# Where the operand sums of the second token half are formed, in a hybrid decoder layer

## The chip, the cores and the metric

One core of a Trainium2 chip runs the whole layer. The metric is the device time of one execution in microseconds (us). The program gives work to five engines, each of which takes its own instructions in order: PE (TensorE, the matmuls), DVE (VectorE), ACT (ScalarE), POOL (GpSimd) and SP (SyncE, which issues most transfers here). Transfers, once issued, run on DMA engines beside all of them.

## What is computed

A decoder layer on 2048 tokens of width 1024, all in float32: a norm, an input projection, two recurrent mixers, an output projection with residual, a second norm, a feed-forward block with residual, and a last norm. Only the feed-forward block matters here:

```python
D_MODEL = 1024; SEQ = 2048; D_FF = 2816; CONV_WIDTH = 3
def _conv_ffn(h, w_up, conv_w, conv_b, w_down):
    u = h @ w_up                                   # (2048, 1024) @ (1024, 5632)
    u = lax.conv_general_dilated(u, conv_w[:, None, :], window_strides=(1,),
        padding=[(CONV_WIDTH - 1, 0)], ..., feature_group_count=C) + conv_b
    gate, val = jnp.split(u, 2, axis=-1)
    return (jax.nn.silu(gate) * val) @ w_down      # (2048, 2816) @ (2816, 1024)
# in the layer:
x = x + _conv_ffn(_rmsnorm(x, norm2_w[l]), w_up[l], conv_w[l], conv_b[l], w_down[l])
return _rmsnorm(x, final_norm_w)
```

## The kernel before

**Products in three parts.** Each float32 operand is split into a rounded high part (an ACT cast, L244 or L237) and the rest (a DVE subtraction, L245 or L238). A product of two operands is three matmuls per tile (`mm3`, L258 to L262), so each operand costs PE nothing and ACT and DVE one pass each.

**Seven products for eight.** Both projections of the feed-forward block multiply 2 by 2 blocks with seven products instead of eight. This needs sums and differences of blocks as operands. Four sums are made from four tiles with four DVE operations, each using the one before.

**Up-projection.** `run` (L1324) goes through 2 token halves with 22 row groups of the hidden width each: iterations n = 0 to 43, and 44 which only finishes. An iteration has seven products (`prod`, L1344) of 12 matmuls on 128 by 512 tiles. The last two of an iteration (`late`, L1398) are done after the first product of the next iteration, and then the convolution and the gate follow. The gated product of row group fb, `y`, is stored to DRAM by two transfers (L1423) into `gd_[2h]` and `gd_[2h+1]`, one per block of 512 tokens. Weights come through six buffers named `uraw`, split operands through five named `uwh` and `uwl`.

**Work on the side.** `side` is a list of small pieces: loads, DVE operations with their stores, and empty pauses. `aside` (L1290) takes one piece after each product, seven per iteration. `four` (L1250) appends a group of five pieces: load four tiles (`raw_`, six buffers named `br`), pause, two DVE operations, two DVE operations and four stores, pause. The pieces made so are the norm of the later tokens, sums of the hidden state, sums of the down-projection's weights (`Tw`), and from iteration 23 on the sums of the first token half's gated product: 11 row groups (KH = 11), each reading rows kk and 11+kk of `gd_[0]` and `gd_[1]` and writing row group kk of the four tensors `Sg[0][0..3]`.

**Down-projection.** `steps` lists 143 steps (half g, product p, row group kk), each 12 matmuls on two operands of 128 by 512, 256 KB each. The first three run at the end of the up-projection (`down_start`). In the loop from L1489, step s issues the loads for step s+4 (six buffers named `draw`), splits the operands of step s+2 and does its matmuls. At the end of each product results are added to the residual rows `xt3`, which are loaded ahead (L1449), and finished rows are normalised and stored to `out` (L1465). The loads and stores all stand in SP's queue, in order. The second half's products read `Sg[1]`. Its sums are made in the same loop:

```python
sums_at = {KH + 5 * j + 2: j for j in range(KH)}
...
            if s_ in sums_at:
                g_sums(d_raw("sraw"), 1, sums_at[s_])
```

`g_sums` (L191) loads four tiles into six buffers named `sraw`, does the four DVE operations (L194 to L197) and issues four stores (L199). The steps are 13, 18, ... 63; steps 66 on belong to the second half, and `Sg[1]` is read from its second product on.

A scheduling layer puts the instructions of each engine into a fixed order when the program is built, and sets the waits from what each reads and writes, DRAM tensors too. PE's products keep the code's order; loads and vector operations may move against each other.

Of the kernel before, what the change touches and what calls it, by code (L numbers as in the profile page):

```python
# [21 lines left out]
KD = D // P  # L22
# [3 lines left out]
NFF = FF // P  # L26
# [35 lines left out]
def tile_layer(ctx, tc, consts, x, norm1_w, w_in, hg_lb_logits, hg_norm_w, rw_shift_mu, rw_w0, rw_w2,  # L62
# [5 lines left out]
    dma = nc.sync.dma_start  # L68
# [25 lines left out]
    def pst(name):  # L94
        return pools["ps"].tile([P, 512], F32, tag="mm", name=name, bufs=8)
# [39 lines left out]
    with tc.tile_pool(name="vp", bufs=1, reuse_waits="tile") as vp, tc.tile_pool(name="ps0", bufs=1, space=PSUM, reuse_waits="tile") as pools["ps"]:  # L135
        rows = vp.tile([P, P], F32, name="rows")
        V.memset(rows, 0.0)
        n = 0
# [39 lines left out]
    h2d = [dp.tile([D, BLK], F32, name=f"h2d{b}") for b in range(NBLK)]  # L178
    gd_ = [dp.tile([FF, BLK], F32, name=f"gd{b}") for b in range(NBLK)]
    KH = NFF // 2  # L180
    Sg = [[dp.tile([KH * P, BLK], F32, name=f"Sg{g}{i}") for i in range(4)] for g in range(2)]
    Tw = [dp.tile([KH * P, BLK], F32, name=f"Tw{i}") for i in range(4)]

    def krows(t_, q, kk):

        return t_[(q * KH + kk) * P:(q * KH + kk + 1) * P, :]

# [3 lines left out]
    def g_sums(tile_, g, kk):  # L191
# [6 lines left out]
        for i, t_ in enumerate((a22, a11, a21, a12)):  # L198
# [4 lines left out]
          ("b", 3, (1, 1)))  # L203
    steps = [(g, p, kk) for g in range(2) for p in range(7) for kk in range(KH) if (g, p) != (0, 1)]
    M2 = [dp.tile([P, BLK], F32, name=f"M2{i}") for i in range(4)]
# [7 lines left out]
    def d_matmuls(accs, s_, lhs, rhs, i):  # L213
        g, p, kk = steps[s_]
        is_ = slice(i * P, (i + 1) * P)
        mm3(accs[i], (lhs[0][:, is_], lhs[1][:, is_]), rhs, kk == 0 and p in (0, 1, 3), kk == KH - 1, True)
    Ts = [[dp.tile([BLK, BLK], F32, name=f"Ts{h}{i}") for i in range(4)] for h in range(2)]
# [40 lines left out]
    def mm3(acc, lhs, rhs, first, last, skip=False):  # L258
        (lh, ll), (rh, rl) = lhs, rhs
        TE.matmul(acc, lh, rh, start=first, stop=False, skip_group_check=skip)  # L260
        TE.matmul(acc, lh, rl, start=False, stop=False, skip_group_check=skip)  # L261
        TE.matmul(acc, ll, rh, start=False, stop=last, skip_group_check=skip)  # L262
# [844 lines left out]
    with ExitStack() as c2:  # L1107
# [11 lines left out]
        def raw_(src):  # L1119
            t_ = hr.tile([P, BLK], F32, tag="br", name="br", bufs=6)  # L1120
            if src is not None:
                loader[0](t_, src)
            return t_
# [20 lines left out]
        with tc.tile_pool(name="op", bufs=1, reuse_waits="tile") as op_:  # L1144
# [46 lines left out]
            for dh in range(2):  # L1191
                accs = [pst("wacc") for _ in range(4)]
                for n, k in enumerate((0, 1, 4, 5, 2, 3, 6, 7)):
# [16 lines left out]
                    if dh == 1 and 2 <= n:  # L1210
                        for j in range(2):
                            q = 2 * (n - 2) + j
# [9 lines left out]
        with tc.tile_pool(name="up", bufs=1, reuse_waits="tile") as up:  # L1222
# [2 lines left out]
            V.memset(halo, 0.0)  # L1225


            side = []

            def norm_last(b, i2):  # L1230

                xt = []

                def load():
                    for q in range(2):
                        xt.append(up.tile([P, D], F32, tag="xt2", name="xt2", bufs=2))
                        dma(xt[q], x1d[b][(i2 * 2 + q) * P:(i2 * 2 + q + 1) * P, :])

                def scale(q):
                    V.tensor_scalar_mul(xt[q], xt[q], rstd(hr, xt[q], "nst", "br", 6))  # L1240

                def evict(k, tp, w):
                    t_ = hr.tile([P, 256], F32, tag="br", name="h2", bufs=6)
                    act(t_, tp, AF.Copy, scale=w)
                    dma(h2d[b][k * P:(k + 1) * P, i2 * 256:i2 * 256 + 256], t_)

                g = transposed(xt, "n2", lambda: pst("tp"), evict)
                side.extend([load, None, lambda: scale(0), lambda: scale(1), None] + [lambda: next(g)] * KD)

            def four(srcs, make, dsts):  # L1250

                ts = []
                side.extend([lambda: ts.extend(raw_(v) for v in srcs), None,
                             lambda: make(ts, 0), lambda: (make(ts, 1), [dma(d, t_) for d, t_ in dsts(ts)]), None])

            def t_make(ts, part):
                b11, b12, b21, b22 = ts
# [16 lines left out]
            QB = [(q, b) for q in range(2) for b in range(2)]  # L1274
            t_out = lambda row: lambda ts: [(row(i), ts[j]) for i, j in enumerate((0, 3, 1, 2))]
            s_out = lambda row: lambda ts: [(row(i), ts[j]) for i, j in enumerate((3, 0, 2, 1))]
# [3 lines left out]
            for kk in range(4):  # L1280
                four([hsrc(1, q, b, kk) for q, b in QB], t_make, t_out(lambda i, kk=kk: tdst(1, i, kk)))
            for kk in range(KH):
                four([wd_quarter(q, dh, kk) for q, dh in QB], t_make, t_out(lambda i, kk=kk: krows(Tw[i], 0, kk)))
            late_side = len(side)
            for kk in range(KH):
                four([krows(gd_[u], q, kk) for u, q in QB], s_make, s_out(lambda i, kk=kk: krows(Sg[0][i], 0, kk)))
            side.reverse()
            late_side = len(side) - late_side

            def aside(n):  # L1290

                if side and (1 <= n < NFF - 2 or n > NFF) and (n > NFF or len(side) > late_side):
                    f = side.pop()
                    if f is not None:
                        f()

# [132 lines left out]
    with tc.tile_pool(name="dn", bufs=1, reuse_waits="tile") as dn:  # L1429
        ops, xts, pend, m2 = {}, {}, [], {}  # L1430
        N = len(steps)

        def d_raw(tag):
            def f(src):
                t_ = dn.tile([P, BLK], F32, tag=tag, name=tag, bufs=6)
                dma(t_, src)
                return t_
            return f

        raws = {}  # L1440

        def load(s_):
            if s_ < N and s_ not in raws:
                g, p, kk = steps[s_]
                raws[s_] = d_loads(s_, d_raw("draw"))
                if p == 0 and kk in (4, 6, 8, 10) or p == 2 - g and kk in (1, 3, 5, 7):
                    u, i = (0, kk // 2 - 2) if p == 0 else (1, kk // 2)
                    t_ = dn.tile([P, D], F32, tag="xt3", name="xt3", bufs=12)
                    dma(t_, x1d[2 * g + u][i * P:(i + 1) * P, :])  # L1449
                    xts[(g, u, i)] = t_  # L1450

        def take(s_):
            if s_ < N:
                ops[s_] = (split(dn, raws[s_][0], [P, BLK], "da", 5), split(dn, raws[s_][1], [P, BLK], "db", 5))
                raws.pop(s_)

        def add(g, u, dh, i, acc):
            t_ = xts[(g, u, i)][:, dh * BLK:(dh + 1) * BLK]
            V.tensor_add(t_, acc, t_)

        def finish(g, u, i):
            t_ = xts.pop((g, u, i))
            V.scalar_tensor_tensor(t_, t_, rstd(dn, t_, "fst"), fw, ALU.mult, ALU.mult)
            t0 = (2 * g + u) * BLK + i * P
            dma(out[0, t0:t0 + P, :], t_)  # L1465

        def evict(g, p, accs, i):

            if p in (0, 2, 4):
                add(g, *((0, 0), None, (0, 1), None, (1, 1))[p], i, accs["a"][i])  # L1470
            if p == 1:
                pend.append(lambda: add(g, 0, 0, i, accs["b"][i]))
            if p == 4:
                pend.append(lambda: add(g, 1, 1, i, accs["b"][i]))
            if p == 5:
                pend.append(lambda: (add(g, 1, 0, i, accs["a"][i]), finish(g, 1, i)))
            if p == 6:
                pend.append(lambda: (add(g, 0, 1, i, accs["b"][i]), finish(g, 0, i)))

        fw = None  # L1480
        accs = {"a": dstate["accs"]}
        for s_ in range(3, 7):
            load(s_)
        take(3)
        take(4)
        fw = dn.tile([P, D], F32, name="fw")
        dma(fw, final_norm_w.unsqueeze(0).broadcast_to([P, D]))
        sums_at = {KH + 5 * j + 2: j for j in range(KH)}
        for s_ in range(3, N):  # L1489
            g, p, kk = steps[s_]  # L1490
            if "b" not in accs and p == 3:
                accs["b"] = [pst("db") for _ in range(4)]
            load(s_ + 4)
            take(s_ + 2)
            acc = accs[DP[p][0]]
            if s_ < N - 3:
                lhs, rhs = ops.pop(s_)
                for i in range(4):
                    d_matmuls(acc, s_, lhs, rhs, i)
                    if kk == KH - 1:  # L1500
                        evict(g, p, accs, i)
            elif s_ == N - 1:
                for i in range(4):
                    for q in range(N - 3, N):
                        d_matmuls(acc, q, *ops[q], i)
                    evict(g, p, accs, i)
            if pend and kk != KH - 1:
                pend.pop(0)()
            if (g, p) == (0, 2):
                if kk == 0:  # L1510
                    for i in range(4):
                        m2[i] = dn.tile([P, BLK], F32, tag="m2", name="m2", bufs=4)
                        dma(m2[i], M2[i])
# [37 lines left out]
```

## Time and profile before

| | us |
|---|---|
| median of 3 runs | 2756.31 (2747.66 to 2756.97) |
| profiled execution | 2742.4 |
| its span, first to last instruction | 2740.6 |
| PE busy | 2638.4 (96%) |
| DVE busy | 1899.1 (69%) |
| ACT busy | 1349.5 (49%) |

The page's 40 slices of 68.5 us each, in tenths of busy time, and what the transfers moved:

```profile
PE   7999999989999999999899999999999999998998
DVE  4857656575456664757568789988898787667656
DMA  8655544355653546933674467746763222999865
```

The up-projection runs from about slice 21 to slice 34, the down-projection from slice 34 to the end. A digit of PE does not mean peak: a matmul of 128 by 512 is shown some 390 ns long, while the next one starts earlier. In the views of groups, a line like L244 or L1436 belongs to a helper and holds many tiles; the names before and after the arrow (`draw<-Sg`) tell which.

### The profile page before, as it was taken

To read this page: it belongs to the slowest core of one execution; us is meant where nothing else is said; L and a number is where in the kernel's file an instruction comes from. 1 tells how busy PE (TensorE), PEld (TensorE's weight loads), DVE (VectorE), ACT (ScalarE), POOL (GpSimd) and SP (SyncE) were. 2 spreads that over 40 slices of the span, in tenths; PEclk is the share of its full clock that TensorE was granted. 3 is DMA by queue.
4 is the path that set the end of the run, shared out by engine and by line. 5 is a ranking of instruction groups with operands and counts; after the bars stand their busy time and mean duration, and the time that the engine had idled before them with its cause. 6 is when DMAs were issued, how large, how long until landed. Compare 5 with 4: busy or idle time off the path is not lost.

```text
span 2740.6 us, 47945 instructions
## 1 busy us (share of the span) xinstructions
PE 2638.4 (96%) x18059; PEld 2098.8 (77%) x18059; DVE 1899.1 (69%) x3665; ACT 1349.5 (49%) x2168; POOL 368.9 (13%) x660
## 2 busy tenths in 40 slices
PE   7999999989999999999899999999999999998998
PEld 6777777767777767778677888887888888776887
DVE  4857656575456664757568789988898787667656
ACT  5455443444544444443356754556445554445544
POOL 6433222212222113222100000000000000000000
PEclk9999999999999999999999999999999999999999
DMA  8655544355653546933674467746763222999865
GB/s 303 199 166 166 165 136 130 117 148 183 214 167 111 148 152 204 311 123 119 182 265 139 140 199 258 240 148 207 264 232 113 90 86 76 323 333 327 298 194 184
DMA packets 365437, 517.87 MB, mean 189 GB/s; under 512 B 97439, under 2 KB 194069, under 8 KB 365205
## 3 DMA queue, kind: packets, MB, share of 16 engines
q1 hardware_dynamic: 313265, 345.39, 38.9%
q0 software_dynamic: 51872, 169.41, 19.0%
q8 instruction: 142, 2.33, 0.4%
q14 instruction: 90, 0.74, 0.1%
q10 hardware_dynamic: 68, 0.02, 0.0%
HBM read 376.27 MB, written 138.41 MB: 188 GB/s over the span
## 4 chain that ended last, share of the span: by engine, by line
PE 68%; DMA 10%; DVE 8%; issue 6%; ACT 5%; SPq 1%; POOL 1%; DVEq 0%; ACTq 0%; POOLq 0%
PE pj L260 8%; PE pj L261 7%; PE pj L262 7%; PE ua L262 5%; PE ua L260 5%; PE ua L261 5%; PE ud L262 2%; PE ud L260 2%; PE ud L261 2%; PE da L261 2%; PE da L260 2%; PE da L262 2%; PE hg L971 2%; DMA woraw<-in_w_out_dram 2%; PE ub L262 1%
## 5 line engine op out<-in xcount | busy, mean ns | idle before, releaser
L260 PE MATMUL pj<-hh,wh 128*128 128x512 f32 x960 | 403.5, 420 | 1.4 <-ACT hh L117 0.7
L261 PE MATMUL pj<-hl,wh 128*128 128x512 f32 x960 | 379.5, 396 | 0.0
L262 PE MATMUL pj<-hh,wl 128*128 128x512 f32 x960 | 379.2, 395 | 0.0
L260 PE MATMUL ua<-Bh,uwh 128*128 128x512 f32 x704 | 276.8, 393 | 4.9 <-ACT uwh L244 3.1
L262 PE MATMUL ua<-Bh,uwl 128*128 128x512 f32 x704 | 275.1, 391 | 0.2 <-DVE uwl L245 0.2
L261 PE MATMUL ua<-Bl,uwh 128*128 128x512 f32 x704 | 274.7, 390 | 0.0
L260 PEld LDWEIGHTS pj<-hh,wh 128*128 128x128 f32 x960 | 181.7, 189 | 54.7 <-issue 11.8
L261 PEld LDWEIGHTS pj<-hl,wh 128*128 128x128 f32 x960 | 182.0, 190 | 39.4 <-issue 6.2
L262 PEld LDWEIGHTS pj<-hh,wl 128*128 128x128 f32 x960 | 181.6, 189 | 39.8 <-issue 0.4
L244 ACT CAST uwh<-uraw 128x512 fp32r<-128x512 f32 x220 | 134.1, 617 | 124.6 <-PE ua L261 58.5
L245 DVE TENSOR_TENSOR uwl<-uraw,uwh 128x512 fp32r<-128x512 f32 x220 | 147.0, 686 | 48.7 <-ACT uwh L244 48.5
L244 ACT CAST dah<-draw 128x512 fp32r<-128x512 f32 x140 | 87.0, 622 | 184.7 <-DMA draw<-Sg 60.0
L245 DVE TENSOR_TENSOR dal<-draw,dah 128x512 fp32r<-128x512 f32 x140 | 96.6, 690 | 103.8 <-ACT dah L244 103.5
L260 PEld LDWEIGHTS ua<-Bh,uwh 128*128 128x128 f32 x704 | 132.6, 188 | 33.6 <-ACT uwh L244 3.5
L262 PEld LDWEIGHTS ua<-Bh,uwl 128*128 128x128 f32 x704 | 132.5, 188 | 28.4 <-DVE uwl L245 0.6
L261 PEld LDWEIGHTS ua<-Bl,uwh 128*128 128x128 f32 x704 | 132.7, 188 | 27.0
L260 PE MATMUL ud<-Bh,uwh 128*128 128x512 f32 x352 | 137.9, 392 | 0.3 <-ACT uwh L244 0.3
L262 PE MATMUL ud<-Bh,uwl 128*128 128x512 f32 x352 | 137.1, 390 | 0.0
L261 PE MATMUL ud<-Bl,uwh 128*128 128x512 f32 x352 | 137.0, 389 | 0.0
L261 PE MATMUL da<-dbl,dah 128*128 128x512 f32 x340 | 133.3, 392 | 1.3 <-DVE dbl L245 1.3
L262 PE MATMUL da<-dbh,dal 128*128 128x512 f32 x340 | 132.3, 390 | 0.0
L260 PE MATMUL da<-dbh,dah 128*128 128x512 f32 x340 | 124.6, 392 | 6.5 <-ACT dbh L244 6.5
(570 smaller groups left out, 6050.3 us busy)
## 6 DMA issues: line engine op xcount, KB each, us to landing
uraw<-in_w_up_dram SPq DMA_DIRECT2D x176, 256.0 KB, 3.4
woraw<-in_w_out_dram POOLq DMA_DIRECT2D x96, 256.0 KB, 3.5
draw<-Sg SPq DMA_DIRECT2D x88, 256.0 KB, 3.4
draw<-Tw SPq DMA_DIRECT2D x88, 256.0 KB, 3.4
gd<-y SPq DMA_DIRECT2D x86, 256.0 KB, 3.0
xt<-x1d SPq DMA_DIRECT2D x32, 512.0 KB, 7.2
wraw<-in_w_in_dram POOLq DMA_DIRECT2D x60, 256.0 KB, 4.7
br<-in_w_down_dram SPq DMA_DIRECT2D x58, 256.0 KB, 3.8
```

The source lines that it names most:

```text
L244: S.copy(hi, src)
L245: V.tensor_sub(lo, src, hi.bitcast(F32))
L260: TE.matmul(acc, lh, rh, start=first, stop=False, skip_group_check=skip)
L261: TE.matmul(acc, lh, rl, start=False, stop=False, skip_group_check=skip)
L262: TE.matmul(acc, ll, rh, start=False, stop=last, skip_group_check=skip)
L971: TE.matmul(o, kt[:, t0:t0 + 64], qs, start=True, stop=True, tile_position=(0, e * 64))
```

## The change

Eight of the 11 row groups of the second half's sums (`EARLY = 8`, row groups 0 to 7) become pieces on the side in the up-projection, one group per iteration from n = 35 to 42. Row group kk needs rows kk and 11+kk of `gd_[2]` and `gd_[3]`; row 11+kk is stored during iteration 34+kk, and the group starts at 35+kk. For this each piece on the side carries the first iteration in which it may run. The other three groups stay in the down-projection, at steps 13, 19 and 25. The four operations, four loads and four stores of a group are the same in both places, with `br` buffers instead of `sraw`.

```diff
+    EARLY = 8
...
-            side = []
+            side, first_at = [], [1]
+
+            def aside_of(fs):
+
+                side.extend((first_at[0], f) for f in fs)
...
-                side.extend([lambda: ts.extend(raw_(v) for v in srcs), None,
-                             lambda: make(ts, 0), lambda: (make(ts, 1), [dma(d, t_) for d, t_ in dsts(ts)]), None])
+                aside_of([lambda: ts.extend(raw_(v) for v in srcs), None,
+                          lambda: make(ts, 0), lambda: (make(ts, 1), [dma(d, t_) for d, t_ in dsts(ts)]), None])
...
-            late_side = len(side)
-            for kk in range(KH):
-                four([krows(gd_[u], q, kk) for u, q in QB], s_make, s_out(lambda i, kk=kk: krows(Sg[0][i], 0, kk)))
+            for g in range(2):
+                for kk in range(({0: KH, 1: EARLY})[g]):
+                    first_at[0] = NFF + 1 + g * (KH + 1 + kk)
+                    four([krows(gd_[2 * g + u], q, kk) for u, q in QB], s_make,
+                         s_out(lambda i, g=g, kk=kk: krows(Sg[g][i], 0, kk)))
             side.reverse()
-            late_side = len(side) - late_side
...
-                if side and (1 <= n < NFF - 2 or n > NFF) and (n > NFF or len(side) > late_side):
-                    f = side.pop()
+                if side and n >= side[-1][0] and not NFF - 2 <= n <= NFF:
+                    f = side.pop()[1]
...
-        sums_at = {KH + 5 * j + 2: j for j in range(KH)}
+        sums_at = {KH + 6 * j + 2: EARLY + j for j in range(KH - EARLY)}
```

The order of PE's instructions does not change. Three places where others move; lines after the change are some five higher than before.

DVE in iteration 35 of the up-projection, from the split of `s1` (an operand) to the convolution of the iteration before (`y1`, `y0`). Before:

```order
L245 TENSOR_TENSOR uwl_21759<-s1_21736,uwh_21758 128x512
L245 TENSOR_TENSOR uwl_21776<-uraw_21644,uwh_21775 128x512
L1415 SCALAR_TENSOR_TENSOR y1_21707<-cv_21561,cvt_14639,y1_21707 128x1024
L1407 TENSOR_TENSOR cg_21560<-ud_21563,m2_21601 128x512
L1416 SCALAR_TENSOR_TENSOR y1_21707<-cv_21561,cvt_14639,y1_21707 128x1024
```

Now:

```order
L246 TENSOR_TENSOR uwl_21769<-s1_21744,uwh_21768 128x512
L1273 TENSOR_TENSOR br_21671<-br_21669,br_21671 128x512
L1274 TENSOR_TENSOR br_21669<-br_21665,br_21669 128x512
L246 TENSOR_TENSOR uwl_21792<-uraw_21644,uwh_21791 128x512
L1276 TENSOR_TENSOR br_21665<-br_21671,br_21665 128x512
L1421 SCALAR_TENSOR_TENSOR y1_21715<-cv_21561,cvt_14639,y1_21715 128x1024
L1413 TENSOR_TENSOR cg_21560<-ud_21563,m2_21601 128x512
L1422 SCALAR_TENSOR_TENSOR y1_21715<-cv_21561,cvt_14639,y1_21715 128x1024
L1277 TENSOR_TENSOR br_21667<-br_21667,br_21665 128x512
```

The four operations of a group (`br`) stand between the splits and inside the convolution; what was there before keeps its order. The first of them waits for the loads of its tiles, and all behind it waits with it.

SP at the same place, around the store of row 11 of the gated product (`gd2`, `gd3` from `y0_21547`). Before:

```order
L1139 DMA uraw_21797<-in_w_up_dram 128x4x128
L1423 DMA gd2_156<-y0_21547 128x512
L1423 DMA gd3_157<-y0_21547 128x512
L1139 DMA uraw_21799<-in_w_up_dram 128x4x128
```

Now:

```order
L1140 DMA uraw_21813<-in_w_up_dram 128x4x128
L1429 DMA gd2_156<-y0_21547 128x512
L1429 DMA gd3_157<-y0_21547 128x512
L1140 DMA uraw_21815<-in_w_up_dram 128x4x128
L1123 DMA br_21667<-gd2_156 128x512
L1123 DMA br_21669<-gd3_157 128x512
L1123 DMA br_21671<-gd3_157 128x512
L1123 DMA br_21836<-gd2_156 128x512
L1259 DMA Sg10_162<-br_21671 128x512
L1259 DMA Sg12_164<-br_21669 128x512
L1140 DMA uraw_21817<-in_w_up_dram 128x4x128
L1259 DMA Sg11_163<-br_21665 128x512
```

The loads of the group follow the store of the row that two of them read, with one weight load between, and a weight load stands behind the stores of the sums.

SP in the down-projection, at the sixth product of the first half (`gd1` with `Tw3`). Before, with one of the groups of sums:

```order
L1436 DMA sraw_24325<-gd2_156 128x512
L1436 DMA sraw_24327<-gd2_156 128x512
L1436 DMA sraw_24329<-gd3_157 128x512
L1436 DMA sraw_24331<-gd3_157 128x512
L1436 DMA draw_24341<-gd1_155 128x512
L1436 DMA draw_24343<-Tw3_169 128x512
L1436 DMA draw_24366<-gd1_155 128x512
L1436 DMA draw_24368<-Tw3_169 128x512
L199 DMA Sg10_162<-sraw_24331 128x512
L199 DMA Sg11_163<-sraw_24325 128x512
L199 DMA Sg12_164<-sraw_24329 128x512
L199 DMA Sg13_165<-sraw_24327 128x512
```

Now:

```order
L1455 DMA xt3_25156<-x1d2_148 128x1024
L1442 DMA draw_24377<-gd1_155 128x512
L1442 DMA draw_24379<-Tw3_169 128x512
L1442 DMA draw_24405<-gd1_155 128x512
L1442 DMA draw_24407<-Tw3_169 128x512
L1442 DMA draw_24430<-gd1_155 128x512
L1442 DMA draw_24432<-Tw3_169 128x512
```

Operand loads follow one another, and the loads of the second half's first residual rows (`xt3` from `x1d2`) have moved ahead of the output stores, which they stood among before.

More of the change, by code (lines that the diff above doesn't have):

```diff
@@ L1247, in norm_last @@
                 g = transposed(xt, "n2", lambda: pst("tp"), evict)
-                side.extend([load, None, lambda: scale(0), lambda: scale(1), None] + [lambda: next(g)] * KD)
+                aside_of([load, None, lambda: scale(0), lambda: scale(1), None] + [lambda: next(g)] * KD)
             def four(srcs, make, dsts):
                 ts = []
-                side.extend([lambda: ts.extend(raw_(v) for v in srcs), None,
-                             lambda: make(ts, 0), lambda: (make(ts, 1), [dma(d, t_) for d, t_ in dsts(ts)]), None])
+                aside_of([lambda: ts.extend(raw_(v) for v in srcs), None,
+                          lambda: make(ts, 0), lambda: (make(ts, 1), [dma(d, t_) for d, t_ in dsts(ts)]), None])
             def t_make(ts, part):
```

## The prediction

> **What bounds the kernel now.** I read the busy time by stage first, because the page's 96% for PE is a mean over stages that differ. Stretches of the last part, in us from the span's start (columns: PE, PEld, DVE and ACT busy time with instruction counts, POOL, granted clock, DMA share, GB/s):
>
> ```profile
> 2330.00:2400.00 70.00, 66.24 (x286) 53.28 (x286) 46.40 (x71) 32.35 (x52) 1.11 (x2) 1.00 0.91 327
> 2400.00:2480.00 80.00, 78.69 (x339) 62.67 (x338) 56.96 (x89) 35.07 (x56) 0.00 (x0) 1.00 0.94 333
> 2480.00:2560.00 80.00, 71.42 (x295) 55.27 (x294) 56.09 (x82) 41.73 (x84) 0.00 (x0) 0.98 0.94 338
> 2560.00:2720.00 160.00, 160.00 (x707) 132.49 (x706) 94.82 (x145) 75.17 (x138) 0.00 (x0) 1.00 0.68 219
> ```
>
> The down-projection is PE-bound from 2560 on and transfer-bound before. The count of matmuls shows the loss better than the busy time, since a matmul is shown 389 ns long but follows its predecessor sooner. The spacing comes from an up-projection iteration, and the row under it is the stretch in which the up-projection already forms sums, those of the first half:
>
> ```profile
> 2142.12:2161.16 19.04, 19.04 (x86) 15.77 (x85) 14.78 (x22) 9.69 (x15) 0.00 (x0) 1.00 0.27 84
> 1940.00:2060.00 120.00, 120.00 (x531) 99.38 (x530) 114.77 (x173) 60.63 (x90) 0.00 (x0) 1.00 0.76 252
> ```
>
> An iteration is 7 products of 12 matmuls, 84 (the row counts two that cross an edge twice): 19.04/84 = 0.2267 us each. Then 70 us hold 308.8 and 80 us 352.9, and edges add about 1.2 (160 us hold 705.9, the row has 707). Short are 24.0 matmuls in the first stretch, 15.1 in the second, 59.1 in the third: **5.4, 3.4 and 13.4 us, together 22.2**. The view of PE's waits names their end, though it shows only 13.6 us, the idle time that outlasts a matmul's shown length:
>
> ```profile
> PE da L260 <- ACT dbh L244: 6.5, 5, 1.8
> PE db L260 <- ACT dbh L244: 4.5, 4, 2.6
> PE db L261 <- DVE dbl L245: 1.3, 2, 1.0
> PE da L261 <- DVE dbl L245: 1.3, 3, 0.8
> ```
>
> So PE waits for the casts of down-projection operands. Behind those casts stand transfers, and behind the transfers SP's queue; the second row here is SP's own wait, for the sums:
>
> ```profile
> ACT dah L244 <- DMA draw<-Sg: 58.0, 25, 5.0
> SPq L199 <- DVE sraw L194: 32.9, 11, 3.5
> ```
>
> One group of sums in SP's order of time shows how it goes: four loads to 2501.7, a few operand loads, then a wait until DVE has the sums at 2507.18, then four stores, and only at 2510.25 the next operand. ACT and PE in the same microseconds, below it, wait in their turn:
>
> ```profile
> 2498.89 2.79 SPq L1436 DMA_DIRECT2D sraw<-gd  x4
> 2507.18 2.98 SPq L199 DMA_DIRECT2D Sg<-sraw  x4
> 2510.25 0.41 SPq L1436 DMA_DIRECT2D draw<-Sg  x1
> ```
>
> ```profile
> 2507.15 0.62 ACT L244 CAST dah<-draw 128x512 fp32r<-128x512 f32 x1 [4.42 <-DVE sraw L194]
> ```
>
> ```profile
> 2508.50 0.96 PE L260 MATMUL db<-dbh,dah 128*128 128x512 f32 x3 [2.63 <-ACT dbh L244]
> ```
>
> The amounts agree. The issues of this stage, 256 KB each, and the span of the loads for sums (durations min/median/max ns, first and last start):
>
> ```profile
> sraw<-gd SPq DMA_DIRECT2D x44, 256.0 KB, 5.1
> Sg<-sraw SPq DMA_DIRECT2D x44, 256.0 KB, 2.7
> ```
>
> ```profile
> L1436 SPq DMA_DIRECT2D sraw<-gd x44: 319/424/1168, 2362.2 to 2515.9; - x44
> ```
>
> A step is 12 matmuls, 2.72 us, and needs two operands, 0.524 MB: 193 GB/s. A group moves eight tiles, 2.10 MB, every five steps (13.6 us): 154 GB/s. The 347 GB/s exceed what the stage moves, 333 to 338, even before output stores and residual loads come in. So the lead is used up and the loss is worst late.
>
> **The change part by part.** *Eight groups leave the down-projection*: 32 subtractions or additions on DVE, 32 loads and 32 stores, 16.8 MB. Three stay, at steps 13, 19 and 25. The first stands where it stood (2362); the third comes 12 steps or 33 us later, about 2395, so its stores end near 2407.
> - To 2400 the load is as before: of the 5.4 us I take back nothing. Spacing of six steps (129 GB/s for the sums, 322 in all) could give 2.0 back, no more, since the last up-projection work and the first group cause most of it.
> - 2400 to 2480: 3.4 us. What is left, 193 GB/s, is the rate at which the stretch behind 2560 ran without a loss. 0.5 us stays for the third group's tail: 2.9 back.
> - 2480 to 2560: 13.4 us. Output stores (a burst of four from 2485, one from 2528, 512 KB each) and residual loads stay, among the operand loads:
>
> ```profile
> 2485.21 0.34 SPq L1465 DMA_DIRECT2D out_dram<-xt  x1
> 2527.97 0.45 SPq L1465 DMA_DIRECT2D out_dram<-xt  x1
> ```
>
> ```profile
> xt<-x1d SPq DMA_DIRECT2D x16, 512.0 KB, 6.5
> out_dram<-xt SPq DMA_DIRECT2D x16, 512.0 KB, 4.2
> ```
>
> Each kind passes without a loss where it stands alone in this trace; the two stretches that show it, with an issue of each:
>
> ```profile
> 2700.00:2720.00 20.00, 20.00 (x90) 16.57 (x89) 15.29 (x21) 13.13 (x30) 0.00 (x0) 1.00 0.79 262
> 2560.00:2580.00 20.00, 20.00 (x90) 16.54 (x89) 13.41 (x20) 11.79 (x20) 0.00 (x0) 1.00 0.93 317
> ```
>
> ```profile
> 2708.47 2.14 SPq L1465 DMA_DIRECT2D out_dram<-xt  x2
> 2561.87 0.42 SPq L1449 DMA_DIRECT2D xt<-x1d  x1
> ```
>
> Together, around the turn to the second half, they make four stores, four loads and eight steps' operands, 8.4 MB in 21.8 us or 385 GB/s; at 338 that is 3.1 us late. The six operand buffers hold three steps, 8.2 us, so I take 1.0 of a possible 0 to 4.6 (the earlier burst, four stores in four steps, is 4.2 MB in 10.9 us, 1.5 us late): 12.4 back.
>
> *The eight groups enter the up-projection*, one in each of iterations 35 to 42. DVE has 19.04 - 14.78 = 4.26 us free there; four operations, each 0.60 us behind the one before (rows 2142.58 and 2143.18 below), fill 2.4. Transfers rise by 2.10 MB/19 us = 110 GB/s to 194. That is less than the quoted stretch with first-half sums carried (a group each 12 us, DVE at 114.77 of 120, 252 GB/s) with PE at 120.00 of 120. As throughput it is hidden.
>
> What that stretch does not show is a fresh source. The new loads read row 11+kk of the gated product, which the iteration before stored: SP, which is in order, must hold them until the store has landed, and DVE, in order too, holds behind the first subtraction the split of the next operand and the convolution that makes the next store. That is a loop. Its pieces from one of the steady iterations (SP, then DVE, then PE), and the times to landing, of the loads beside the first half's sums and of the gated stores over the whole run:
>
> ```profile
> 2161.73 0.82 SPq L1423 DMA_DIRECT2D gd<-y  x2
> ```
>
> ```profile
> 2142.58 0.68 DVE L1384 TENSOR_TENSOR s<-uraw 128x512 f32<-128x512 f32 x1
> 2143.18 0.69 DVE L245 TENSOR_TENSOR uwl<-uraw,uwh 128x512 fp32r<-128x512 f32 x1
> 2150.90 0.69 DVE L245 TENSOR_TENSOR uwl<-uraw,uwh 128x512 fp32r<-128x512 f32 x1 [2.02 <-ACT uwh L244]
> 2152.67 1.28 DVE L1415 SCALAR_TENSOR_TENSOR y<-cv,cvt,y 128x1024 f32<-128x1024 f32 x1 [1.08 <-ACT y L117]
> ```
>
> ```profile
> 2161.11 0.39 PE L260 MATMUL ua<-Bh,uwh 128*128 128x512 f32 x1
> ```
>
> ```profile
> DMA to landing us min/median/max: 2.7/3.9/5.4
> DMA to landing us min/median/max: 2.1/3.0/5.4
> ```
>
> From the store's issue: second store 0.4, landing 3.0, two more load issues 0.7, landing 2.7 to 3.9, four operations 2.4, the split 0.6, and from the convolution's first row to the next store 2161.73 - 2152.67 = 9.1. Sum 18.9 to 20.1 against 19.04: at most 1.1 us per iteration, 8.5 over eight. The split done at 2151.6 is that of the product that starts at 2161.11 (PE takes the products in the code's order), so PE has 9.5 us of lead and should not feel it. I charge 0.5 us, for a lag carried into the last iterations; bounds 0 and, at the longest landings (5.4 and 5.4: 24.0 us a turn), 8 x 4.9 - 9.5 = 30. The Trainium skill, "DMA: Bandwidth & Descriptors", section "Two DMAs through the same engine are not ordered", speaks against the change here: a load of what a store wrote must wait for that store's completion. By it alone the 18.9 to 20.1 stand; without such a wait the turn would be about 3 us shorter and the charge 0. No row before shows the pair back to back.
>
> The six loads for the first three down-projection steps also wait for buffers now, and move from 2061 into the last two iterations before it. They are used at 2316; a landing of 3.9 us fits. Cost 0, and 3.9 us if that cover went.
>
> ```profile
> L1122 SPq DMA_DIRECT2D br<-gd x48: 319/382/766, 1901.6 to 2061.5; - x48
> ```
>
> ```profile
> L260 PE MATMUL da<-uwh x12: 389/389/389, 2316.1 to 2329.2; 128*128 128x512 f32 x12
> ```
>
> **Sum.** 0 + 2.9 + 12.4 - 0.5 = 14.8, say 15 us. The profiled execution took 2742.4 (span 2740.6 and 1.8 around it), so 2727; the median of the runs shown is 13.9 higher, 2756.3, so **2741**.
>
> **The rivals.** *The bursts keep the wait* (smaller gain): output stores wait for DVE in SP's queue just as the sums' stores do, and the 4.6 us stay, with 2 us lost above. Then 3.4 - 0.5 + 13.4 - 4.6 - 2 = 9.7: 2733 profiled, 2747. For it: the loss is largest in the stretch that holds both bursts. Against: the two stretches without loss.
>
> *The loop governs the up-projection* (slower): with both landings at 5.4, PE loses 30 us in iterations 35 to 42 and gains 15 later: 2757 profiled, 2771. It decides once 8 x excess - 9.5 exceeds 15, an excess of 3.1 us, a store and a load whose landings take 8.9 us together, where the medians make 6.9. For it: the first group of the first half held DVE 4.04 us, as its semaphore row shows. Against: that was one of two waits in eleven groups, in the busier stretch.
>
> ```profile
> L1268 DVEq EVENT_SEMAPHORE  x11: 49/50/4042, 1925.0 to 2048.3; - x11
> ```
>
> *It does not do what it says*: a scheduler could have put the groups elsewhere. The order rows shown with the change exclude nearly all of that; no difference, 2756.
>
> **How the numbers follow.** About 0.5%, 13.8 us, is what a measurement of this kernel tells from no change. Forecast 0.66, with gains of 12 to 19 us, a sixth of it (0.11) under 13.8; bursts 0.25; loop 0.07; nothing 0.02. Faster 0.55, same 0.11 + 0.25 + 0.02 = 0.38, slower 0.07. Range: below, 19 us of gain (2737) and the 9 us by which the shown runs differ, taken by three quarters: 2730. Above, the bursts' 2747 and the same 7: 2754. That leaves out the loop and some of each tail.
>
> **What would show it.** Right: 2400 to 2560 at 353 matmuls per 80 us and nearer 220 than 338 GB/s; SP's wait for sums down from 11 to 3; the loss before 2400 still 4 to 6 us; iterations 35 to 42 still 19.04 us long, DVE near 17.2 us busy, its waits for the new loads up to 2 us each and PE silent. Wrong: PE short in those iterations, a wait of casts for operands that outlives the sums beside the output stores, or a loss before 2400 that goes too (then the gain is over 17).

## The result and the profile after

| | before | changed |
|---|---|---|
| median, us | 2756.66 (22 runs, 2747.66 to 2771.03) | 2746.52 (22 runs, 2737.13 to 2760.15) |
| profiled execution, us (span) | 2742.4 (2740.6) | 2744.17 (2742.4) |

The ratio is 0.9966, 95% interval 0.9953 to 0.9979: faster by 9.4 us (5.8 to 13.0), two thirds of the 15 us forecast. That is less than the 0.5% (13.8 us) which the prediction named as the least that a measurement tells from no change, but the interval leaves no change out.

The two profiled executions by themselves would say that the change costs 1.8 us. They must be compared by stage. The store of row 11 of the second half's gated product, the first that an early group waits for, is issued at 2142.69 before and at 2150.41 now: the execution with the change was 7.7 us late before anything that was changed had run. From that store on I use two lengths. The first goes from the store to the first matmul `da<-uwh` of the down-projection (173.4 us before), the second from that matmul to the end of the span (2740.6 - 2316.1 = 424.5 us before).

The down-projection by stretches in the changed kernel, columns as before (PE, PEld, DVE, ACT, POOL, clock, DMA share, GB/s):

```profile
2330.00:2400.00 70.00, 65.12 (x280) 51.72 (x279) 42.67 (x63) 31.80 (x50) 1.10 (x2) 1.00 0.80 279
2400.00:2480.00 80.00, 79.83 (x351) 65.16 (x350) 53.64 (x84) 38.52 (x64) 0.00 (x0) 1.00 0.88 293
2480.00:2560.00 80.00, 80.00 (x355) 66.26 (x353) 55.33 (x80) 44.40 (x91) 0.00 (x0) 1.00 0.79 270
```

339 and 295 matmuls have become 351 and 355 where PE at its pace makes 352.9 and some 1.2 at the edges: nothing is lost from 2400 to 2560 but three matmuls. The first stretch is about as short of matmuls as it was. The stage begins 16.3 us later in this trace, so the same clock times are not the same steps; counted in stretches of 80 us from the stage's first matmul, the three hold 323, 351 and 354 matmuls, where before 329, 339 and 296 did. That is 1.4 us lost, then 2.7 and 13.1 gained. SP's wait for sums, 32.9 us in 11 times before, in the view of SP's queue:

```profile
SPq L200 <- DVE sraw L195: 9.7, 3, 3.5
```

The first product of the down-projection, from the view of its line:

```profile
L261 PE MATMUL da<-uwh x12: 389/389/389, 2332.4 to 2345.5; 128*128 128x512 f32 x12
```

From there to the end are 2742.4 - 2332.4 = 410.0 us, **14.5 less than before**; the prediction's terms for this stage made 15.3. But from the store at 2150.41 to that product are 182.0 us, **8.6 more than before**, where 0.5 had been charged. 14.5 - 8.6 = 5.9, plus 1.8 is the 7.7 of the early part; the runs' 9.4 with their interval from 5.8 hold the 5.9.

The eight turns with an early group, from that store to the store of row 19, in the changed kernel, and one of them:

```profile
2150.41:2312.93 162.52, 157.55 (x689) 128.57 (x689) 137.31 (x201) 76.15 (x112) 0.00 (x0) 1.00 0.57 189
2170.60:2190.81 20.21, 20.21 (x90) 16.71 (x90) 17.82 (x27) 9.67 (x14) 0.00 (x0) 1.00 0.60 188
```

and the same eight iterations before:

```profile
2142.69:2295.01 152.32, 152.32 (x673) 126.13 (x673) 118.17 (x169) 77.56 (x112) 0.00 (x0) 1.00 0.26 83
```

Eight iterations of 19.04 us have become eight of 20.3; the loop is 162.52 - 152.32 = 10.2 us behind at the end. No engine is full: DVE is busy 137.31 of 162.52 us, transfers move 189 GB/s. The waits of this stretch in the changed kernel (us in all, times, longest):

```profile
ACT y L117 <- DVE cg L1413: 29.6, 8, 6.3
DVE br L1273 <- DMA br<-gd: 23.6, 8, 4.5
ACT uwh L245 <- DVE s L1391: 18.6, 8, 2.8
PE ua L261 <- ACT m L117: 6.5, 6, 1.6
```

Of these only the first is in the view of the same stretch before:

```profile
ACT y L117 <- DVE cg L1407: 9.5, 9, 1.1
```

In each of the eight turns DVE stands still for the new loads, 3 us on average, and everything behind it on DVE is late. One turn in the chain of waits (start, length, what):

```profile
2211.18 4.28 DMA gd<-y
2215.46 0.02 issue
2215.47 0.32 SPq L1123
...
2216.36 3.79 DMA br<-gd
2220.15 0.02 issue
2220.17 0.70 DVE br L1273
...
2223.52 1.20 DVE y L1421
```

The store takes 4.28 us to land, SP then issues the loads, the last of which lands at 2220.15, 8.97 us after the store's issue. The prediction had 0.4 + 3.0 + 0.7 + 2.7 to 3.9, that is 6.8 to 8.0. The Trainium skill, "DMA: Bandwidth & Descriptors", section "Two DMAs through the same engine are not ordered", says that the issuing engine has to wait for the completion of the first of two such transfers before it issues the second. The trace agrees: SP issues the load 0.02 us behind the store's landing.

But SP waits for the store in four of the eight turns only, as the view of its queue from 2150 to 2320 shows:

```profile
SPq L1123 <- DMA gd<-y: 6.7, 4, 2.9
SPq L1140 <- DVE uraw L1397: 6.1, 4, 1.5
```

In the other four the group's loads stand behind a weight load (L1140) that waits until DVE has freed its buffer (L1397). From the store's issue to the group's first operation are 7.6 to 9.0 us in the turns of the first kind and 8.0 to 9.5 in those of the second, 8.4 on the mean of all eight.

How this reaches PE is seen at the end of the same turn, behind the next store (2232.49). ACT in order of time, then PE:

```profile
2234.35 0.62 ACT L245 CAST uwh<-s 128x512 fp32r<-128x512 f32 x1 [2.65 <-DVE s L1391]
2234.88 0.59 ACT L117 ACTIVATE m<-ua 128x512 f32<-128x512 f32 x1
```

```profile
2235.52 0.50 PE L261 MATMUL ua<-Bh,uwh 128*128 128x512 f32 x1 [1.62 <-ACT m L117]
```

`s` is the sum of weight tiles for a coming product, and it stands on DVE behind the convolution. ACT, in order, waits 2.65 us for it ahead of a cast; behind that cast stands the copy of PE's accumulator (`m<-ua`, 2234.88), and PE's next product into `ua` starts only when the copy is done.

### The profile page after: what moved, and what is told of

Same layout as the page of the kernel before. It is cut to its first block, busy times and chain, and to the rows that moved or that the text cites. A ratio compares the mean times of both kernels' runs of the same rounds, so it can differ in the third digit from the quotient of the medians.

```text
span 2742.4 us, 47952 instructions
## 1 busy us (share of the span) xinstructions
PE 2636.5 (96%) x18059; PEld 2098.3 (77%) x18059; DVE 1897.7 (69%) x3665; ACT 1345.5 (49%) x2168; POOL 367.4 (13%) x660
## 4 chain that ended last, share of the span: by engine, by line
PE 69%; DMA 10%; DVE 9%; issue 6%; ACT 4%; SPq 1%; POOL 1%; DVEq 0%; ACTq 0%; POOLq 0%
PE pj L261 8%; PE pj L262 7%; PE pj L263 7%; PE ua L261 4%; PE ua L263 4%; PE ua L262 4%; PE da L261 2%; PE da L262 2%; PE da L263 2%; PE ud L263 2%; PE ud L262 2%; PE ud L261 2%; PE db L262 2%; PE db L263 2%; PE hg L972 2%
## 5 line engine op out<-in xcount | busy, mean ns | idle before, releaser
L261 PEld LDWEIGHTS pj<-hh,wh 128*128 128x128 f32 x960 | 181.9, 190 | 54.4 <-issue 12.5
L261 PE MATMUL da<-dbh,dah 128*128 128x512 f32 x340 | 131.3, 390 | 4.2 <-ACT dbh L245 4.2
```

## The experiments

All ratios are to the kernel before, run on the same chip beside them. "Lost" is the first length less 173.4, "down" the second.

| | ratio (95% interval) | lost, us | down, us |
|---|---|---|---|
| kernel before | 1 | 0 | 424.5 |
| changed kernel | 0.9966 (0.9953 to 0.9979) | 8.6 | 410.0 |
| e1_old_rows | 0.9923 (0.9899 to 0.9948) | 0.0 | 407.9 |
| e2_late_make | 0.9935 (0.9914 to 0.9956) | 0.1 | 410.6 |
| e6_late_make_again | 0.9925 (0.9906 to 0.9944) | 0.1 | 408.5 |
| e3_shift1 | 0.9972 (0.9957 to 0.9988) | 8.5 | 410.8 |
| e4_pause2 | 0.9973 (0.9956 to 0.9990) | 10.1 | 409.6 |
| e7_early4 | 0.9941 (0.9919 to 0.9962) | 5.2 | 410.9 |
| e12_late_make_4 | 0.9946 (0.9932 to 0.9961) | 0.0 | 416.2 |
| e5_spread | 0.9931 (0.9913 to 0.9948) | 0.0 | 406.0 |
| e8_pool_all | 1.0087 (1.0058 to 1.0116) | 0.1 | 457.4 |
| e9_six_steps | 1.0036 (1.0020 to 1.0051) | 0.0 | 437.3 |
| e10_seven_steps | 1.0021 (1.0004 to 1.0039) | 0.0 | 436.2 |
| e11_stores_on_pool | 0.9977 (0.9964 to 0.9989) | 0.1 | 421.2 |

### What holds the up-projection

**e1_old_rows**: the early groups read the first token half's rows, which were stored long before. The number of loads, operations and stores stays.

```diff
-                    four([krows(gd_[2 * g + u], q, kk) for u, q in QB], s_make,
+                    four([krows(gd_[u], q, kk) for u, q in QB], s_make,
```

> The eight early groups read the first half's gated rows, which were stored long before, and write them where the second half's sums belong; so the second half of the output is wrong, and every load, operation and store is there as in the change. Theory L (the loop store, load, subtraction, convolution, store of each iteration is longer than PE's 19.04 us): the loads no longer wait for a fresh store, iterations 35 to 42 are 19.04 us again, PE shows no wait for ACT there, and the time is about 15 us under before (ratio 0.9945, 6 us under the change). Rival W (32 more DVE operations and 16.8 MB more transfers in that stage cost what they cost, wherever the rows are from): iterations 35 to 42 stay near 20.3 us, ratio 0.9966 as the change.

Turns of 19.04 us and nothing lost; the eight turns from the same store on:

```profile
2152.55:2304.87 152.32, 152.32 (x673) 126.17 (x673) 128.08 (x185) 77.53 (x112) 0.00 (x0) 1.00 0.42 138
```

The work itself is free, as the prediction had it; the fresh source costs the 8.6 us. The scheduling layer used the freedom, though: the eight groups' first operations run from 2082.27 to 2213.90, four turns sooner than in the changed kernel, with their loads issued 9 us or more ahead. Only four of the eight are in the row above, which is why it shows 138 GB/s. The turns with the other four are 19.04 us or less as well. All four operations still stand ahead of the convolution on DVE, and none of them waits. So this run shows that without a wait nothing is lost, and not by itself which wait of the changed kernel cost the time.

**e2_late_make**: one more pause between a group's loads and its operations, and the first operation is ordered on DVE behind the gate's multiplication, from which the next store comes.

```diff
-                aside_of([lambda: ts.extend(raw_(v) for v in srcs), None,
+                aside_of([lambda: ts.extend(raw_(v) for v in srcs)] + [None] * wait +
...
+                    tc.add_manual_dep(i_.ins, gated[-1].ins.name, NOSYNC, reason="after the gate")
```

> Output right. The same groups and rows, but one more pause, and the first operation of a group is held on DVE behind the gating product of its iteration, so that the wait for the loads no longer stands ahead of the convolution. Theory L: the loop is cut on DVE's side, its wait for the loads is under 0.5 us an iteration, iterations 35 to 42 take 19.04 us, time 13 to 16 us under before (ratio 0.994 to 0.9955). Rival W: 20.3 us an iteration and ratio 0.9966. Rival S (SP's queue, in which loads that wait for a store hold up the weight loads): the queue is as before, so 20.3 us stay as well, and DVE's splits or ACT's casts wait for uraw.

The eight turns and one of them:

```profile
2152.70:2305.01 152.31, 152.31 (x673) 126.12 (x673) 134.32 (x197) 78.23 (x112) 0.00 (x0) 1.00 0.57 188
2171.73:2190.77 19.04, 19.04 (x85) 15.77 (x85) 17.08 (x26) 9.79 (x14) 0.00 (x0) 1.00 0.60 193
```

The same 188 GB/s and the same operations, 17.08 us of DVE in a turn, and not one wait of DVE for the new loads, which now have some 12 us before the group's first operation (issued until 2197.22, used at 2209.70). The loads still stand behind the store on SP; only the convolution no longer stands behind the loads on DVE. So the loads' place behind the store on SP is not what cost the time. (The stores of the sums have moved on SP too, from among the weight loads to behind the next gated store; what they cost at their old place is not shown apart.) This kernel is faster than both, before and after: 17.9 us under before, and 20.7 in the second measurement (e6).

> The same kernel as e2_late_make, once more beside e5_spread: ratio near 0.9935 (0.9914 to 0.9956).

**e3_shift1** lets each group start an iteration later in the code; **e4_pause2** adds the pause alone, without the order on DVE.

```diff
-                    first_at[0] = NFF + 1 + g * (KH + 1 + kk)
+                    first_at[0] = NFF + 1 + g * (KH + 2 + kk)
```

> Output right. Every early group may start one iteration later (36 to 43). The loads still stand right behind the fresh store in SP's order, but only two of the four operations stand ahead of the convolution, the other two behind the gating product. Theory L: the turn is shorter by two operations and by the split that stood between, some 1.8 us of the 20.3, so 18.5, under 19.04: no loss in the up-projection, 12 to 15 us under before (ratio 0.9945 to 0.9956), unless the six loads of the first down-projection steps, now behind the last group, come late (up to 4 us). Rival W: as the change, 0.9966.

> Output right. One more pause in each early group, nothing else; the scheduler then puts the fourth operation behind the convolution in every other iteration only. Theory L: the turn is 0.6 us shorter in every other iteration, so 20.0 on the mean, 2.4 of 10 us of lag less: 10 to 12 us under before (ratio 0.9957 to 0.9964). Rival W: 0.9966. This is the run in which the two lie closest.

Both missed: turns of 20.5 us in both, and losses of 8.5 and 10.1 us. The chain of waits of e3_shift1, one turn:

```profile
2238.18 0.68 DVE uwl L246
2238.86 0.61 DVE uraw L1397
2239.49 0.38 SPq L1140
2239.97 4.13 DMA br<-gd
2244.22 0.70 DVE br L1273
...
2245.64 1.20 DVE y L1421
```

In e3_shift1 the scheduling layer left the first group's loads where they were, right behind the store of row 11 (2154.87, the store 2151.99), and the others likewise. So the rows are as fresh as in the changed kernel, and SP waits for the store five times, 6.1 us. What moved are two of the four operations, from ahead of the convolution to behind the gate. The store is not in the chain of this turn, and yet DVE waits eight times for the loads ahead of the convolution, 26.9 us in all (it was 23.6). In SP's queue the group's load follows a weight load (L1140) that waits until DVE has freed a buffer (L1397). DVE's work, SP's weight load, the group's load, DVE's convolution: that is a loop as well, and as long. It is the loop of the second kind of turns of the changed kernel above. The two operations that moved are still in it: they run at 2235.78 and 2236.98, ahead of the work on DVE for which the weight load waits. A later start in the code or a pause gives nothing while the first operation stays ahead of the convolution; what e2 changed was that place.

**e7_early4**: `EARLY = 4`, four groups early and seven in the down-projection.

> The changed kernel with four groups in the up-projection and seven in the down-projection (steps 13, 19, ... 49). If a turn is 20.3 us as measured and PE has only the difference of the two measured lags as lead (10.2 of the loop, 8.6 of PE: 1.6 us), four turns put the loop 5.1 us behind and PE loses about 3.5 us before the down-projection. If PE had the 9.5 us of lead that the prediction reckoned with, it would lose nothing here, and the 8.6 us of eight groups would come from the last one or two turns alone. In the down-projection seven groups instead of three: 2480 to 2560 near 350 matmuls per 80 us, 2400 to 2480 some 340.

The four turns with a group, and the four after them:

```profile
2153.91:2236.88 82.97, 80.30 (x353) 65.87 (x353) 68.69 (x101) 38.31 (x56) 0.00 (x0) 1.00 0.59 194
2236.88:2311.40 74.52, 72.91 (x322) 60.08 (x321) 58.97 (x85) 38.60 (x56) 0.00 (x0) 1.00 0.26 84
```

Four turns are 82.97 - 4 x 19.04 = 6.8 us too long, the four others 1.64 us short of 76.16, and PE lost the rest, 5.2. So the lead that PE has over this loop is 1.6 us, not 9.5; the changed kernel gives the same (10.2 of the loop less 8.6 of PE). The surprise is the other stage: with seven groups left in it, it took 410.9 us, only 0.9 more than with three.

**e12_late_make_4** joins the two, four early groups with the loop cut.

> The kernel of e2_late_make with four groups in the up-projection instead of eight. With the loop cut the up-projection loses nothing (iterations 19.04 us), and the down-projection keeps what e7_early4 had (410.9 us from its first matmul to the end): the time of e2, ratio 0.9925 to 0.9940, where e7 with the loop had 0.9941 and 5.2 us lost.

Nothing lost in the up-projection, and a time that this comparison can't tell from that of e2, nor from that of e7, which lost 5.2 us there. Its traced execution was the slowest of its ten, with 416.2 us in the down-projection; whether seven remaining groups cost 1 us or 6 stays open.

### What holds the down-projection

The prediction gave two reasons, SP's wait for each group and the 347 GB/s that the operands and sums ask for. Moving groups away removes both, so the change itself can't tell them apart.

**e9_six_steps** and **e10_seven_steps**: the kernel before, its eleven groups wider apart.

```diff
-        sums_at = {KH + 5 * j + 2: j for j in range(KH)}
+        sums_at = {KH + 6 * j + 2: j for j in range(KH)}
```

(e10: `7 * j + 6`.)

> The kernel before with its eleven groups in the down-projection, one every six steps (13, 19, ... 73) instead of every five; nothing moves into the up-projection. If the stage is bound by what it moves, 193 GB/s of operands and 129 of sums are 322, under the 333 to 338 that ran: the loss of 3.4 us in 2400 to 2480 falls to 1 to 2, and that of 13.4 in 2480 to 2560 to 5 to 9, since sums and output stores still meet there: 5 to 10 us in all, ratio 0.9965 to 0.9982. If it is the waits of SP's queue for each group, their number is still eleven and the gain is 0 to 3 us: ratio 0.9990 to 1.0000.

> The same with a group every seven steps, from step 6 to step 76: 193 + 110 = 303 GB/s. Bandwidth: 2 to 4 us more gained than by six steps, ratio 0.9955 to 0.9972, although the first group comes nearer to the start of the stage, where the loss is not made by the sums. Waits: still eleven, 0 to 4 us gained, ratio 0.9985 to 1.0000.

Both slower than before, by 0.4 and 0.2% with intervals clear of no change, which neither theory had. e9 by stretches:

```profile
2400.00:2480.00 80.00, 76.77 (x335) 62.30 (x334) 55.61 (x87) 37.17 (x60) 0.00 (x0) 1.00 0.92 314
2480.00:2560.00 80.00, 71.34 (x282) 54.76 (x281) 52.51 (x76) 37.53 (x76) 0.00 (x0) 0.94 0.92 320
2560.00:2720.00 160.00, 155.59 (x675) 127.91 (x674) 90.88 (x143) 68.64 (x119) 0.00 (x0) 0.98 0.69 225
```

Less is moved, 314 and 320 GB/s for 333 and 338, and more matmuls are missing: 335 for 339, 282 for 295, and 675 for 707 in a stretch that had lost none. Its last groups run until 2572 instead of 2526, among the second burst of output stores and the residual loads. So e9 by itself does not refute the bytes: it asks for fewer on the whole, but there its sums come on top of the burst. (The stage begins 8.7 us later in this trace than before; its whole length is 12.8 us more.) Not all of the missing matmuls are waits. From 2480 to 2560 PE is busy as long as before, 71.34 us for 71.42, and does 13 matmuls fewer: the granted clock is 0.94 for 0.98. In this stage it is below 1.00 only in slices of 10 us with a wait of PE or right behind one, in e9 down to 0.72 from 2550 to 2560, and before 0.83 from 2510 to 2520.

e7_early4 and e9 have their first seven groups at the same steps, 13 to 49. e7 took 410.9 us for the stage (e12, with the same seven, 416.2) and e9 437.3: the other 21 to 26 us come with the last four groups. Nor do the output stores and residual loads lose anything alone, as the changed kernel shows. The two lose where they meet.

SP waits for sums as often as before, and DVE waits for the groups' loads, 14.0 us where it was 8.7; one of these waits:

```profile
SPq L199 <- DVE sraw L194: 34.8, 11, 4.9
```

```profile
2541.25 0.68 DVE L245 TENSOR_TENSOR dbl<-draw,dbh 128x512 fp32r<-128x512 f32 x1
2544.34 0.69 DVE L194 TENSOR_TENSOR sraw<-sraw 128x512 f32<-128x512 f32 x1 [2.40 <-DMA sraw<-gd]
```

**e11_stores_on_pool** and **e8_pool_all**: the kernel before with the sums' stores, or their stores and loads, issued by POOL.

```diff
-            dma(krows(Sg[g][i], 0, kk), t_)
+            nc.gpsimd.dma_start(krows(Sg[g][i], 0, kk), t_)
```

(e8 also: `(nc.gpsimd.dma_start if tag == "sraw" else dma)(t_, src)`.)

> The kernel before with only the stores of the eleven groups issued by POOL; their loads stay in SP's queue. SP then never waits for a sum, and DVE gets the sums' loads as early as before. If the order in SP's queue makes the loss, most of it goes: first down-projection matmul to the end 405 to 414 us (before: 424.5, with loads on POOL too: 457.4). If bandwidth makes it, 420 to 428 us, at 333 to 338 GB/s between 2400 and 2560.

> The kernel before, with the loads and stores of the eleven groups of sums in the down-projection issued by POOL instead of SP, so that no operand load stands behind a store that waits for a sum. If bandwidth makes the loss (347 GB/s and more wanted, 333 to 338 moved), it stays: first down-projection matmul to the end 420 to 426 us (before: 424.5), 333 to 338 GB/s between 2400 and 2560. If the order in SP's queue makes it, most of the 22 us come back: 405 to 412.

e11 by stretches, and the one long wait of PE in it:

```profile
2400.00:2480.00 80.00, 69.83 (x299) 57.32 (x298) 54.03 (x87) 32.45 (x53) 11.90 (x22) 0.94 0.96 346
2480.00:2560.00 80.00, 78.95 (x346) 64.48 (x345) 59.04 (x87) 43.66 (x88) 8.10 (x15) 1.00 0.97 353
```

```profile
PE da L260 <- DVE xt L1459: 10.2, 1, 10.2
```

In the last of these stretches 346 matmuls run where before had 295, and 353 GB/s are moved: 338 was not the ceiling. Both bursts of output stores and the last groups lie in this stretch, as they did before. So the bytes are not what cost the 13.4 us there. What e11 took away is SP's wait for the sums, with operand loads behind it, and that is the likely cause; it is argued from one trace, in which the stall told below came first and may have helped. In the stretch ahead 55 matmuls are missing, 12.5 us, of which one stall makes 10.2: DVE waits for a group's load, since SP now issues such loads one by one between operand loads (2449.68 to 2459.61), and PE waits for the additions (`xt`) that stand behind it on DVE:

```profile
2462.38 0.69 DVE L194 TENSOR_TENSOR sraw<-sraw 128x512 f32<-128x512 f32 x1 [4.65 <-DMA sraw<-gd]
```

Another 2 us went with the clock, 0.54 from 2460 to 2470. The first ten matmuls behind the stall take 4.3 us instead of 2.3; three of them:

```profile
2466.83 0.77 PE L260 MATMUL da<-dbh,dah 128*128 128x512 f32 x1 [10.17 <-DVE xt L1459]
2467.40 0.63 PE L261 MATMUL da<-dbl,dah 128*128 128x512 f32 x1
2467.82 0.63 PE L262 MATMUL da<-dbh,dal 128*128 128x512 f32 x1
```

So the time was 6.3 us better than before and not 13.

With the loads on POOL as well, this became the rule. DVE waits 56.4 us in nine times for the groups' loads; one of them:

```profile
2403.56 0.69 DVE L194 TENSOR_TENSOR sraw<-sraw 128x512 f32<-128x512 f32 x1 [8.26 <-DMA sraw<-gd]
```

Three splits of operands come right behind it. The loads' median time to landing rose from 5.1 to 6.2 us, and POOL, in order itself, waited 30.8 us for the sums' stores to land before it could load into their buffers. So e8 doesn't settle bytes against order, for which it was made; it shows a third place for the same wait.

**e5_spread**: e2 with its three remaining groups at steps 26, 37 and 48.

> The kernel of e2_late_make (loop cut) with the three groups that stay in the down-projection at steps 26, 37 and 48 instead of 13, 19 and 25. The sums of the second half are read from step 77 on. If the early groups are what loses matmuls between 2330 and 2400 (280 of 308.8 in the changed kernel, 6.5 us), some 2 to 4 us come back there and none is lost later, since the three groups then stand 30 us apart and the stage has room (272 to 282 of some 338 GB/s): ratio to before 0.9920 to 0.9930, first down-projection matmul to the end about 408. Rival: the loss before 2400 is the start of the stage itself (buffers that the up-projection still holds, residual loads): then nothing comes back and the time is that of e2.

The stretch of 2330 to 2400 has 294 matmuls where e6 beside it has 283, 2.5 us, and the stage is 2.5 us shorter (406.0 for 408.5). The medians, 2739.8 and 2739.0, don't show it. Some 16 matmuls, 3.6 us, are still missing in that stretch, in which no load for sums is issued before 2396.21: this much belongs to the start of the stage, with its seven residual loads.

## Why the prediction was right, and where it was wrong

- **2400 to 2560, 2.9 + 12.4 = 15.3 us**: right in size. Counted from the stage's start the two stretches gained 2.7 and 13.1, the whole stage 14.5, the matmuls are there (351 and 355), SP's waits went from 11 to 3. The GB/s were to be nearer 220 than 338; at 293 and 270 they are so in the second stretch only. That figure left out the bursts which the prediction itself had counted: eight output stores and four residual loads of 0.52 MB from 2480 to 2560 are 79 GB/s beside the operands' 193.
- **Its reason**: half wrong. "So the lead is used up" was argued from 347 GB/s against 338. e11 moved 353 with under 2 us lost. What fits all runs is that the lead is used up where operand work stands behind a group's wait, in SP's queue or on DVE, and the output stores come to it. The moved groups take that away with the bytes, so the sum came out all the same; for this part that is luck. The 13.4 us were also read as waits alone: some 1.5 of them went with the lower clock behind a wait (0.83 from 2510 to 2520).
- **To 2400, nothing back**: right that nothing comes back; 280 matmuls of 310, 6.8 us lost for 5.4 before, and e5 puts the sums' part of it at 2.5 us.
- **The bursts keep the wait**: they did not. No matmul is missing from 2480 to 2560, with output stores and residual loads in it. This rival's 2747 is nearly the measured 2746.5, by chance: what is missing of the forecast gain was lost in the up-projection.
- **The charge of 0.5 us for the up-projection**: this is the step that failed, at "PE has 9.5 us of lead and should not feel it". The loop was seen, with the wait that closes it. Its turn, 18.9 to 20.1, measured 20.3, because the store and the loads took 8.4 us on the mean and not 6.8 to 8.0; in four turns of eight a weight load ahead of them on SP made it so, a wait that the sum did not have. That alone would have cost 0.7 us if the lead had been 9.5 us: eight turns make 10.2. But the lead was read from one operand, whose split stands ahead of the wait on DVE. Others stand behind it: the sums `s` of the weights come after the convolution, ACT waits for them in order, and the copy of PE's accumulator stands behind ACT's cast. That path has 1.6 us (e7). 10.2 - 1.6 = 8.6. The time stayed in the range all the same, because the range was drawn for another loss, that of the bursts, and for the spread of the runs.
- **The rival of the loop** had the mechanism and asked for an excess of 3.1 us a turn, again through the 9.5. With 1.6 us of lead each turn over 19.04 counts almost at once: the 1.27 that came cost 8.6.
- **Waits of up to 2 us for each new load**: 3.0 on average, 4.5 at most. **PE silent**: no.

## What to carry to other kernels

A lead that is read from one operand is no lead of the engine: for every wait that is put on an in-order engine, follow each thing behind it, also the copies on another engine that wait for it in their turn, and take the smallest. Work that waits for fresh data is put behind the instruction that makes the next fresh data (e2: a pause and one ordering edge were worth 17.9 - 9.4 = 8.5 us), since a pause or a later start in the code gained nothing as long as the first operation stood ahead of the convolution (e3, e4). And before bytes are blamed, see whether another run moves more without a loss: here 353 GB/s went with under 2 us lost, and 338 with 13.4.

## What was not expected

- The unchanged part of the program took up to 22 us more or less from one profiled execution to the next: the store of row 11 came between 2142.69 (before) and 2164.76 (e12), mostly near 2153. That is more than this change is worth, and only lengths from a common point can be compared.
- With the sums' stores on POOL, 353 GB/s were moved over 80 us while PE lost under 2 us.
- Two stores of 256 KB and the loads that wait for them took 7.5 to 9 us from the first issue to the last landing, in a stretch that moves 189 GB/s.
